# Stick-breaking attention with one mask pass, a scan on the minus log, and turned weights without zero blocks

## The chip, the cores and the metric

One Trainium2 chip, of which one core is used. The metric is the device time of one execution in microseconds (us). The kernel before was run three times: 2461.14, 2464.58 and 2466.43 us, median 2464.58 us. Engines are named as in the profile: PE is TensorE (PEld its weight loads), DVE is VectorE, ACT is ScalarE, POOL is GpSimd, SP issues the DMAs.

## The reference, cut to what matters

One transformer layer on 2048 tokens of 1024 channels: modulated RMS norm, a projection, three token mixers side by side (attention, causal pooling, spatial gating), an output projection, and a SwiGLU feed-forward part. The change is in the attention alone, which has 8 heads of 64 channels and a window of 512 keys:

```
z = einsum('bqhd,bkhd->bhqk', q_blk, k_blk) * scale
log_rest = where(valid, log_sigmoid(-z), 0.0)
later = cumsum(log_rest, axis=3, reverse=True) - log_rest
w = where(valid, exp(log_rest + z + later), 0.0)
out = einsum('bhqk,bkhd->bqhd', w, v_blk)
```

A key is valid for a query if it lies before it and at most 512 tokens back. `log_rest + z` is `log_sigmoid(z)`, so a weight is the chance of stopping at this key times the chances of having passed all later ones.

## The kernel before, in words

All matrix products are done on values split in a high and a low part, with three products each (`mm3`), or two in the attention, where high and low part stand beside or under each other in one operand. Tokens are worked in 4 groups of 512. First come the projections of each group (`proj_a`, `proj_b`), then for each group the output projection and the feed-forward part (`gate_up`, `down`), whose weights are loaded anew for each group, split on ACT (line 263) and on DVE or POOL (line 265).

The attention is a generator (`attention`) that runs along with this work from about 175 us to 1900 us: `weave` emits a step of it whenever a credit, fed by the estimated time of the products in front, reaches one. So its instructions stand between those of the projections and of the feed-forward part in the queues of all engines. The framework then orders each engine's queue by its own timeline model and places the waits. Each engine works its queue strictly in order.

A step of the attention is `att_front` for one tile of 128 queries: the scores (`z`, lines 674 to 679, PE), a copy to SBUF (`zc`, line 681, ACT), then `log(1 + exp(-|z|))` in three ACT instructions (lines 686 to 688), the sum with `max(z, 0)` (line 690, DVE), two masks of 128 columns on this (lines 693 and 698, POOL; the second only for groups 1 to 3), a scan from the last key to the first (line 704, DVE), the difference of scores and scan (line 707, DVE), the same two masks on that (POOL), and the exponential (line 709, ACT). A tile has 640 keys in groups 1 to 3, and 128 to 512 in group 0. There are 128 tiles: 96 of 640 keys and 8 of each smaller size.

`att_back` takes a pair of query tiles, one step later. It works in rounds of two blocks of 128 keys: the weights are turned by PE into the PSUM tile `tr` (line 735; there is one `tr`), copied by ACT as the high part (line 750), subtracted by DVE as the low part (line 751), and multiplied with the values into `av` (line 757), 256 columns at a time: two query tiles side by side. Where one of the two query tiles doesn't see a key block, its place in `wT` is filled with zeros by POOL (line 739). In such a round the used columns fall in two runs, and copy and subtraction are done once per run. A pair has three rounds in groups 1 to 3, and one or two in group 0: 168 rounds in all, of which 112 have two runs.

Of the kernel before, what the change touches and what calls it, by code (L numbers as in the profile page):

```python
# [9 lines left out]
F32 = mybir.dt.float32  # L10
# [5 lines left out]
P = 128  # L16
# [20 lines left out]
def tile_hybrid_trunk(  # L37
# [51 lines left out]
    def mm(ps, lhsT, rhs, start=True, stop=True):  # L89
        PE.matmul(ps, lhsT=lhsT, rhs=rhs, start=start, stop=stop)  # L90
# [40 lines left out]
    def sig_tail(y, e):  # L131
        """e <- log(1 + exp(-|y|)); y <- min(y, 0) - e; y <- exp(y) = sigmoid(y)."""
# [120 lines left out]
    cnt = [0]  # L253

    def wsplit(raw, hl):
        """hl[:, 0] + hl[:, 1] = raw, exactly."""
# [47 lines left out]
    def to_channels(xts, A, sh, res):  # L304
        """4 tiles [128 tok, 1024] -> 8 tiles [128 ch, hi/lo, 512 tok] of A * x + sh."""
# [20 lines left out]
    def ws_unit(ps, hl, hT):  # L326
        """weight-stationary: ps[128 out ch, 512 tok]."""
        for kc in range(KC):
            mm3(
                ps, (hl[:, 0, kc, :], hl[:, 1, kc, :]), (hT[kc][:, 0], hT[kc][:, 1]), 0, 0, kc == 0, kc == KC - 1  # L330
            )

    def seg_scale(raws, dim):
        """1/rms over the channels of raws (tiles [128 ch, 512]), on every partition."""
# [39 lines left out]
    def start():  # L374
        """h of group 0 and its first products, as sc1 and sh1 become known by quarters of the channels."""
# [101 lines left out]
    def proj_a(g):  # L477
        tok = slice(g * GT, (g + 1) * GT)
        hT = hTs[g]
        # q, k  # L480
# [24 lines left out]
        # v  # L505
# [27 lines left out]
        # pooling  # L533
# [130 lines left out]
    def att_front(g, h, i, qst, kst, koff):  # L664
        """weights of stick breaking of q tile i (of group g): [128 q, keys]."""
# [8 lines left out]
        for l in range(2):  # L674
# [5 lines left out]
        zc = st("zc", [P, 640])  # L680
        ACT.activation(
            out=zc[:, :n].rearrange("p (a b) -> p a b", a=pieces), in_=z[:, :pieces, :nn], func=AF.Copy
        )
        e = st("ee", [P, 640])[:, :n]
        zc = zc[:, :n]
# [3 lines left out]
        sp = e  # L689
        DVE.scalar_tensor_tensor(out=sp, in0=zc, scalar=0.0, in1=e, op0=ALU.max, op1=ALU.add)  # L690

        def masks(t, fill):
            POOL.affine_select(  # L693
# [416 lines left out]
```

## Time and profile before

| | |
|---|---|
| median of three runs | 2464.58 us |
| profiled execution: span from the first to the last instruction | 2463.7 us |
| PE busy | 2352.7 us, 95% |
| PEld busy | 1977.3 us, 80% |
| DVE busy | 1692.1 us, 69% |
| ACT busy | 1362.9 us, 55% |
| POOL busy | 1217.0 us, 49% |
| mean granted clock of PE | 0.986 of full speed |

Of the profiled execution the profile gives no time beside its span. A busy share is the union of an engine's instructions over the span. Matmuls are pipelined: one of 512 columns is listed with 395 ns, but in a row of them the next starts after about 0.23 us (22 in 5.28 us). So a price of a matmul is read from the distance of two starts, not from its listed length. "Idle before" names the instruction whose end released the waiting one.

### The profile page before, as it was taken

The page shows a single profiled execution, that of the slowest core. Times are in us where ns is not written, and L with a number is a line of the kernel's source. Part 1 is how long each engine was busy: PE and PEld are TensorE (multiplying, and loading weights), DVE is VectorE, ACT ScalarE, POOL GpSimd, SP SyncE. Part 2 cuts the span into 40 slices and gives each one's busy share as a digit, 9 for nine tenths or more (in the row PEclk, how much of TensorE's full clock was granted, in tenths as well). Part 3 has the DMA queues.
Part 4 walks back from the last instruction along what each step waited for, and adds up shares of the span by engine and source line. Part 5 has one row for each costly group of instructions (what it writes and reads, how often), then busy time and mean ns, then how long its engine had stood idle before and what let it go on. Part 6 is the DMA issues. An engine that isn't in the chain of part 4 may idle for free.

```text
span 2463.7 us, 32486 instructions
## 1 busy us (share of the span) xinstructions
PE 2352.7 (95%) x11730; PEld 1977.3 (80%) x11730; DVE 1692.1 (69%) x2125; ACT 1362.9 (55%) x2307; POOL 1217.0 (49%) x1157
## 2 busy tenths in 40 slices
PE   5999999999999999998999999889999999999998
PEld 4888979788788888777888888768788878788887
DVE  7577888767876777878877777877775456543435
ACT  5366767656666655656665655566664343433333
POOL 4142533345465455675554555754554456344445
PEclk8999999999999999999999999999999999999999
DMA  8857374554333333433433334334333343433332
GB/s 250 270 167 238 120 244 133 158 165 122 96 97 105 105 104 98 139 121 100 129 115 105 105 102 132 124 98 130 99 103 90 102 146 102 140 95 99 98 100 77
DMA packets 336512, 315.62 MB, mean 128 GB/s; under 512 B 12168, under 2 KB 267870, under 8 KB 336352
## 3 DMA queue, kind: packets, MB, share of 16 engines
q1 hardware_dynamic: 336352, 313.56, 41.3%
q8 instruction: 92, 1.51, 0.2%
q14 instruction: 68, 0.56, 0.1%
HBM read 279.95 MB, written 33.56 MB: 127 GB/s over the span
## 4 chain that ended last, share of the span: by engine, by line
PE 49%; DVE 18%; POOL 11%; issue 10%; ACT 8%; DMA 4%; SPq 1%; POOLq 0%; DVEq 0%; ACTq 0%
PE d L90 45%; POOL b L868 4%; DVE ee L704 3%; DVE hl L265 2%; DVE zc L707 2%; POOL hl L265 2%; PE av L90 2%; ACT hl L263 1%; DMA qst<-q_s 1%; DVE b L301 1%; PE tr L735 1%; DMA b<-in_w_ada_dram 1%; PE z L90 1%; DVE ee L690 1%; POOL b L916 1%
## 5 line engine op out<-in xcount | busy, mean ns | idle before, releaser
L90 PE MATMUL d<-b,hl 128*128 128x512 f32 x5184 | 1254.2, 395 | 8.3 <-DVE b L300 3.2
L90 PEld LDWEIGHTS d<-b,hl 128*128 128x128 f32 x5184 | 961.9, 189 | 208.2 <-DVE b L300 5.0
L90 PE MATMUL d<-hl,b 128*128 128x512 f32 (+1 forms) x4428 | 913.9, 359 | 13.2 <-DVE y L867 12.4
L90 PEld LDWEIGHTS d<-hl,b 128*128 128x128 f32 x4428 | 728.9, 191 | 128.3 <-DVE y L867 15.0
L263 ACT ACTIVATE hl<-raw 128x1024 fp32r<-128x1024 f32 x368 | 387.1, 1054 | 238.0 <-PE d L90 231.0
L265 POOL TENSOR_TENSOR hl<-raw,hl 128x1024 fp32r<-128x1024 f32 x122 | 308.2, 2527 | 325.1 <-ACT hl L263 308.7
L265 DVE TENSOR_TENSOR hl<-raw,hl 128x1024 fp32r<-128x1024 f32 x246 | 336.1, 1368 | 191.9 <-ACT hl L263 185.0
L868 POOL TENSOR_TENSOR b<-b,y 128x512 f32<-128x512 f32 x248 | 388.8, 1576 | 143.4 <-DVE y L867 135.8
L916 POOL TENSOR_TENSOR b<-y,b 128x512 fp32r<-128x512 f32 x88 | 165.0, 1875 | 228.3 <-DVE b L915 223.0
L704 DVE TENSOR_TENSOR_SCAN ee<-ee 128x640 f32<-128x640 f32 (+4 forms) x128 | 204.5, 1598 | 61.8 <-POOL ee L698 54.8
L867 DVE TENSOR_TENSOR y<-d,b 128x512 f32<-128x512 f32 x248 | 167.7, 681 | 91.4 <-PE d L90 88.9
L709 ACT ACTIVATE zc<-zc 128x640 f32<-128x640 f32 (+4 forms) x128 | 85.8, 670 | 257.5 <-POOL zc L698 223.4
L90 PE MATMUL av<-wT,vst 128*128 128x256 f32 x672 | 173.0, 295 | 30.6 <-DVE wT L751 13.4
L693 POOL TENSOR_SCALAR_AFFINE_SELECT zc<-zc 128x128 f32<-128x128 f32 x128 | 81.4, 636 | 221.9 <-DVE zc L707 213.8
L751 DVE TENSOR_TENSOR wT<-tr,wT 128x128 fp32r<-128x128 f32 (+1 forms) x280 | 116.6, 416 | 85.5 <-ACT wT L750 85.2
L90 PEld LDWEIGHTS av<-wT,vst 128*128 128x128 f32 x672 | 122.5, 192 | 59.7 <-DVE wT L751 21.4
L750 ACT ACTIVATE wT<-tr 128x128 fp32r<-128x128 f32 (+1 forms) x280 | 105.8, 378 | 104.4 <-DVE wT L751 71.2
L690 DVE SCALAR_TENSOR_TENSOR ee<-zc,ee 128x640 f32<-128x640 f32 (+4 forms) x128 | 125.5, 981 | 47.9 <-ACT ee L688 47.2
L693 POOL TENSOR_SCALAR_AFFINE_SELECT ee<-ee 128x128 f32<-128x128 f32 x128 | 53.6, 419 | 193.2 <-DVE ee L690 189.6
L907 ACT ACTIVATE y<-d 128x512 f32<-128x512 f32 x88 | 52.3, 594 | 150.8 <-PE d L90 150.7
L707 DVE TENSOR_TENSOR zc<-zc,ee 128x640 f32<-128x640 f32 (+4 forms) x128 | 133.7, 1044 | 2.4
L910 DVE SCALAR_TENSOR_TENSOR y<-d,y 128x512 f32<-128x512 f32 x88 | 60.3, 685 | 84.1 <-ACT y L909 83.7
(187 smaller groups left out, 2248.1 us busy)
## 6 DMA issues: line engine op xcount, KB each, us to landing
raw<-in_w_gate_up_dram SPq DMA_DIRECT2D x176, 512.0 KB, 3.9
raw<-in_w_down_dram SPq DMA_DIRECT2D x88, 512.0 KB, 3.7
raw<-in_w_in_dram SPq DMA_DIRECT2D x72, 512.0 KB, 5.2
b<-in_w_ada_dram SPq DMA_DIRECT2D x48, 512.0 KB, 6.7
raw<-in_w_out_dram SPq DMA_DIRECT2D x32, 512.0 KB, 4.3
b<-in_x_dram SPq DMA_DIRECT2D x28, 512.0 KB, 6.0
kst<-k_s SPq DMA_DIRECT2D x24, 512.0 KB, 4.1
qst<-q_s SPq DMA_DIRECT2D x64, 128.0 KB, 4.3
```

The source lines that it names most:

```text
L90: PE.matmul(ps, lhsT=lhsT, rhs=rhs, start=start, stop=stop)
L263: ACT.activation(out=h, in_=r, func=AF.Copy)
L265: eng.tensor_tensor(out=l, in0=r, in1=h.bitcast(F32), op=ALU.subtract)
L690: DVE.scalar_tensor_tensor(out=sp, in0=zc, scalar=0.0, in1=e, op0=ALU.max, op1=ALU.add)
L693: POOL.affine_select(out=t[:, n - P : n], in_=t[:, n - P : n], pattern=[[-1, P]], compare_op=ALU.is_ge, fill=fill, base=-1, channel_multip ...
L704: DVE.tensor_tensor_scan(out=e[:, ::-1], data0=sp[:, ::-1], data1=sp[:, ::-1], initial=0.0, op0=ALU.add, op1=ALU.bypass)
L707: DVE.tensor_tensor(out=zc, in0=zc, in1=e, op=ALU.subtract)
L750: ACT.activation(out=wT[:, 0, a:b], in_=tr[:, a:b], func=AF.Copy)
L751: DVE.tensor_tensor(out=wT[:, 1, a:b], in0=tr[:, a:b], in1=wT[:, 0, a:b].bitcast(F32), op=ALU.subtract)
L867: DVE.tensor_tensor(out=y, in0=ps, in1=gain[:, cs], op=ALU.mult)
L868: POOL.tensor_tensor(out=x1[t][:, cs], in0=x1[t][:, cs], in1=y, op=ALU.add)
L916: POOL.tensor_tensor(out=a[:, 1], in0=y, in1=a[:, 0].bitcast(F32), op=ALU.subtract)
```

## The change

- The masks are applied once, on the copied scores, before the first of the three ACT instructions, with -1e30 as fill.
- DVE makes `e = min(z, 0) - log(1 + exp(-|z|))`, the log of sigmoid(z), in place of the softplus. One scan then gives the minus log of the weight directly: each step adds the score of the next key and takes away `e` of this key. For this the scores stand in a tile with one more column, which POOL sets to zero (128 x 1), and the scan writes its result over the scores, one column to the right. The separate subtraction is gone, and the exponential has the factor -1.
- In `att_back` the key blocks that both query tiles see come first, with 256 columns, and the blocks that only one of them sees come last, with 128 columns. There are no zero blocks, and no memsets of `wT`. A round is filled up to 512 columns and copied by one ACT and one DVE instruction: of 512, 512 and 256 columns for a pair of groups 1 to 3 (48 pairs), of 384 or of 512 and 384 columns for a pair of group 0 (8 pairs each).

```diff
-    def mm(ps, lhsT, rhs, start=True, stop=True):
-        PE.matmul(ps, lhsT=lhsT, rhs=rhs, start=start, stop=stop)
+    def mm(ps, lhsT, rhs, start=True, stop=True, skip=False):
+        PE.matmul(ps, lhsT=lhsT, rhs=rhs, start=start, stop=stop, skip_group_check=skip)
...
-        zc = st("zc", [P, 640])
-        ACT.activation(
-            out=zc[:, :n].rearrange("p (a b) -> p a b", a=pieces), in_=z[:, :pieces, :nn], func=AF.Copy
+        zt = st("zc", [P, 641])
+        POOL.memset(zt[:, n : n + 1], 0.0)
+        zc = zt[:, :n]
+        ACT.activation(out=zc.rearrange("p (a b) -> p a b", a=pieces), in_=z[:, :pieces, :nn], func=AF.Copy)
+        POOL.affine_select(
+            out=zc[:, n - P : n], in_=zc[:, n - P : n], pattern=[[-1, P]], compare_op=ALU.is_ge, fill=NEG,
+            base=-1, channel_multiplier=1,
         )
+        if g > 0:
+            POOL.affine_select(
+                out=zc[:, 0:P], in_=zc[:, 0:P], pattern=[[1, P]], compare_op=ALU.is_ge, fill=NEG,
+                base=0, channel_multiplier=-1,
+            )
         e = st("ee", [P, 640])[:, :n]
-        zc = zc[:, :n]
         ACT.activation(out=e, in_=zc, func=AF.Abs)
         ACT.activation(out=e, in_=e, func=AF.Exp, scale=-1.0)
         ACT.activation(out=e, in_=e, func=AF.Ln, bias=1.0)
-        sp = e
-        DVE.scalar_tensor_tensor(out=sp, in0=zc, scalar=0.0, in1=e, op0=ALU.max, op1=ALU.add)
-
-        def masks(t, fill):
-            POOL.affine_select(
-                out=t[:, n - P : n], in_=t[:, n - P : n], pattern=[[-1, P]], compare_op=ALU.is_ge, fill=fill,
-                base=-1, channel_multiplier=1,
-            )
-            if g > 0:
-                POOL.affine_select(
-                    out=t[:, 0:P], in_=t[:, 0:P], pattern=[[1, P]], compare_op=ALU.is_ge, fill=fill,
-                    base=0, channel_multiplier=-1,
-                )
-
-        masks(sp, 0.0)
+        DVE.scalar_tensor_tensor(out=e, in0=zc, scalar=0.0, in1=e, op0=ALU.min, op1=ALU.subtract)
+        w = zt[:, 1 : n + 1]
         DVE.tensor_tensor_scan(
-            out=e[:, ::-1], data0=sp[:, ::-1], data1=sp[:, ::-1], initial=0.0, op0=ALU.add, op1=ALU.bypass
+            out=w[:, ::-1], data0=w[:, ::-1], data1=e[:, ::-1], initial=0.0, op0=ALU.add, op1=ALU.subtract
         )
-        DVE.tensor_tensor(out=zc, in0=zc, in1=e, op=ALU.subtract)
-        masks(zc, NEG)
-        ACT.activation(out=zc, in_=zc, func=AF.Exp)
-        return zc
+        ACT.activation(out=w, in_=w, func=AF.Exp, scale=-1.0)
+        return w
     def att_back(g, i0, wq, vst, av):
-        """av[:, pair] += [v_hi | v_lo]^T w^T for q tiles i0, i0 + 1."""
         if g > 0:
-            kts = list(range(i0, i0 + 6))
-            has = lambda kt, i: i <= kt <= i + 4
+            both, one = list(range(i0 + 1, i0 + 5)), [(i0, 0), (i0 + 5, 1)]
             loc = lambda kt, i: kt - i
         else:
-            kts = list(range(0, i0 + 2))
-            has = lambda kt, i: kt <= i
+            both, one = list(range(0, i0 + 1)), [(i0 + 1, 1)]
             loc = lambda kt, i: kt
-        nm = 2 * len(kts)
+        items = [(kt, (0, 1)) for kt in both] + [(kt, (q,)) for kt, q in one]
+        rounds, n = [], 512
+        for kt, qs in items:
+            if n + len(qs) * P > 512:
+                rounds.append([])
+                n = 0
+            rounds[-1].append((kt, qs, n))
+            n += len(qs) * P
         m = 0
-        for b0 in range(0, len(kts), 2):
-            bk = kts[b0 : b0 + 2]
+        for rd in rounds:
             seq[0] += 1
             tr = psa.tile([P, 512], F32, tag="tr", name=f"tr_{seq[0]}", bufs=1)
             wT = st("wT", [P, 2, 512], F32R)
-            lo_c, hi_c = None, None
-            for s, kt in enumerate(bk):
-                for q in range(2):
-                    i = i0 + q
-                    c0 = s * 256 + q * P
-                    if has(kt, i):
-                        PE.transpose(
-                            out=tr[:, c0 : c0 + P], in_=wq[q][:, loc(kt, i) * P : (loc(kt, i) + 1) * P], identity=ident
-                        )
-                    else:
-                        POOL.memset(wT[:, :, c0 : c0 + P].bitcast(F32), 0.0)
-            runs = []
-            for s, kt in enumerate(bk):
-                for q in range(2):
-                    if has(kt, i0 + q):
-                        c0 = s * 256 + q * P
-                        if runs and runs[-1][1] == c0:
-                            runs[-1][1] = c0 + P
-                        else:
-                            runs.append([c0, c0 + P])
-            for a, b in runs:
-                ACT.activation(out=wT[:, 0, a:b], in_=tr[:, a:b], func=AF.Copy)
-                DVE.tensor_tensor(
-                    out=wT[:, 1, a:b], in0=tr[:, a:b], in1=wT[:, 0, a:b].bitcast(F32), op=ALU.subtract
-                )
-            for s, kt in enumerate(bk):
+            for kt, qs, c0 in rd:
+                for j, q in enumerate(qs):
+                    b = loc(kt, i0 + q) * P
+                    w = c0 + (j + 1) * P
+                    PE.transpose(out=tr[:, w - P : w], in_=wq[q][:, b : b + P], identity=ident)
+            ACT.activation(out=wT[:, 0, :w], in_=tr[:, :w], func=AF.Copy)
+            DVE.tensor_tensor(out=wT[:, 1, :w], in0=tr[:, :w], in1=wT[:, 0, :w].bitcast(F32), op=ALU.subtract)
+            for kt, qs, c0 in rd:
+                w = len(qs) * P
+                o = (i0 + qs[0]) * P
                 for l in range(2):
-                    mm(
-                        av[:, (i0 % 4) * P : (i0 % 4) * P + 256], vst[:, kt, :],
-                        wT[:, l, s * 256 : (s + 1) * 256], m == 0, m == nm - 1,
-                    )
                     m += 1
+                    mm(av[:, o : o + w], vst[:, kt, :], wT[:, l, c0 : c0 + w], m == 1, m == 2 * len(items), True)
```

How the queues change is shown at three places. The first is PE at the last round of a pair of group 1; `av` is the sum of weights and values, `z` the scores of a later tile, `tr` the turned weights, and the other rows are other work. Before:

```order
L90 MATMUL z_6643<-kst_6282,qst_6284 128x320 x4
L90 MATMUL aux_6873<-b_6190,wsT 128x256 x2
L90 MATMUL av_5557<-wT_6530,vst_5554 128x256
L90 MATMUL z_6666<-kst_6282,qst_6284 128x320 x4
L90 MATMUL aux_6986<-b_6190,wsT 128x256 x2
L90 MATMUL av_5557<-wT_6530,vst_5554 128x256 x3
L735 MATMUL tr_6761<-ident,zc_6300 128x128 x2
L652 MATMUL aux_7168<-ident,b_5986 128x128 x4
```

And with the change:

```order
L90 MATMUL z_6519<-kst_6168,qst_6170 128x320 x2
L90 MATMUL aux_6739<-b_6076,wsT 128x256 x2
L90 MATMUL aux_6850<-b_6076,wsT 128x256 x2
L90 MATMUL av_5463<-wT_6410,vst_5460 128x128
L90 MATMUL z_6540<-kst_6168,qst_6170 128x320 x4
L652 MATMUL aux_7022<-ident,b_5878 128x128 x4
L90 MATMUL av_5463<-wT_6410,vst_5460 128x128 x3
L734 MATMUL tr_6633<-ident,zc_6186 128x128
```

The four products of the round stand in the same manner, one alone and three in a row, with 128 columns in place of 256.

The second place is ACT at the end of group 0, where `wT` of the last round of a pair is copied; line 778 (760 in the change) splits the queries of the next head as they land. Before:

```order
L687 ACTIVATE ee_4697<-ee_4697 128x512
L709 ACTIVATE zc_4588<-zc_4588 128x384
L750 ACTIVATE wT_4752<-tr_4751 128x256
L688 ACTIVATE ee_4697<-ee_4697 128x512
L778 ACTIVATE qst_4876<-qst_4876 128x512
L750 ACTIVATE wT_4752<-tr_4751 128x128
L498 ACTIVATE b_4795<-d_4770 128x512
L263 ACTIVATE hl_5015<-raw_5013 128x1024
```

And with the change, where line 683 is the copy of the scores, lines 695 to 697 are the three instructions on them, line 706 is the exponential and line 735 the copy of `wT`:

```order
L683 ACTIVATE zc_4622<-z_4619 128x512
L706 ACTIVATE zc_4516<-zc_4516 128x384
L695 ACTIVATE ee_4628<-zc_4622 128x512
L696 ACTIVATE ee_4628<-ee_4628 128x512
L735 ACTIVATE wT_4678<-tr_4677 128x384
L697 ACTIVATE ee_4628<-ee_4628 128x512
L760 ACTIVATE qst_4796<-qst_4796 128x512
L498 ACTIVATE b_4718<-d_4693 128x512
```

The copy of `wT` is one instruction, and it stands ahead of the split of the queries; before, its second half stood behind it.

The third place is POOL in group 1, over two tiles of the attention; line 868 (850 in the change) adds a product to the residual stream, line 265 is a weight split. Before:

```order
L265 TENSOR_TENSOR hl_5983<-raw_5981,hl_5983 128x1024
L868 TENSOR_TENSOR b_5495<-b_5495,y_5874 128x512
L693 AFFINE_SELECT ee_5819<-ee_5819 128x128
L698 AFFINE_SELECT ee_5819<-ee_5819 128x128
L868 TENSOR_TENSOR b_5497<-b_5497,y_5897 128x512
L693 AFFINE_SELECT zc_5817<-zc_5817 128x128
L698 AFFINE_SELECT zc_5817<-zc_5817 128x128
L868 TENSOR_TENSOR b_5499<-b_5499,y_5920 128x512
L868 TENSOR_TENSOR b_5501<-b_5501,y_5966 128x512
L693 AFFINE_SELECT ee_5937<-ee_5937 128x128
L698 AFFINE_SELECT ee_5937<-ee_5937 128x128
```

And with the change:

```order
L681 MEMSET zc_5713 128x1
L681 MEMSET zc_5829 128x1
L265 TENSOR_TENSOR hl_5875<-raw_5873,hl_5875 128x1024
L850 TENSOR_TENSOR b_5407<-b_5407,y_5742 128x512
L685 AFFINE_SELECT zc_5713<-zc_5713 128x128
L690 AFFINE_SELECT zc_5713<-zc_5713 128x128
L850 TENSOR_TENSOR b_5401<-b_5401,y_5768 128x512
L850 TENSOR_TENSOR b_5403<-b_5403,y_5791 128x512
L850 TENSOR_TENSOR b_5405<-b_5405,y_5814 128x512
L685 AFFINE_SELECT zc_5829<-zc_5829 128x128
L690 AFFINE_SELECT zc_5829<-zc_5829 128x128
```

A tile has two masks and a small memset in place of four masks, and the memset of the second tile stands ahead of the masks of the first.

## Rows read from the trace of the kernel before

**Rows 1.** The page's part on engines: busy us (share of the span), instructions.
```profile
PE 2352.7 (95%) x11730; PEld 1977.3 (80%) x11730; DVE 1692.1 (69%) x2125; ACT 1362.9 (55%) x2307; POOL 1217.0 (49%) x1157
```

**Rows 2.** Busy time of each engine in three stretches, granted TensorE clock, DMA share.
```profile
0.00:175.00 175.00, 139.84 (x775) 119.76 (x776) 111.93 (x152) 85.24 (x152) 57.64 (x73) 0.95 0.72 227
175.00:1900.00 1725.00, 1661.22 (x8511) 1401.83 (x8510) 1313.63 (x1647) 1073.05 (x1859) 894.49 (x931) 0.99 0.41 125
1900.00:2463.70 563.70, 551.59 (x2448) 455.72 (x2446) 266.57 (x327) 204.63 (x297) 264.91 (x153) 0.99 0.35 106
```

**Rows 3.** Waits of TensorE: line, for whom, us in total, times, longest.
```profile
PE av L90 <- DVE wT L751: 13.4, 14, 2.5
PE av L90 <- ACT wT L750: 13.2, 9, 3.6
PE d L90 <- DVE y L867: 12.4, 7, 3.8
...
PE z L90 <- ACT zc L681: 6.7, 5, 1.7
```

**Rows 4.** TensorE in order of time, three places: start, length, operation, count.
```profile
390.93 0.23 PE L90 MATMUL z<-kst,qst 128*128 128x128 f32 x1
390.99 0.45 PE L90 MATMUL d<-b,hl 128*128 128x512 f32 x1
...
438.71 0.34 PE L90 MATMUL z<-kst,qst 128*128 128x128 f32 x2
438.88 0.33 PE L90 MATMUL av<-wT,vst 128*128 128x256 f32 x1
...
1202.47 0.52 PE L90 MATMUL av<-wT,vst 128*128 128x256 f32 x3
```

**Rows 5.** The page's groups of instructions: busy us, mean ns of one, idle before.
```profile
L704 DVE TENSOR_TENSOR_SCAN ee<-ee 128x640 f32<-128x640 f32 (+4 forms) x128 | 204.5, 1598 | 61.8 <-POOL ee L698 54.8
...
L90 PE MATMUL av<-wT,vst 128*128 128x256 f32 x672 | 173.0, 295 | 30.6 <-DVE wT L751 13.4
...
L751 DVE TENSOR_TENSOR wT<-tr,wT 128x128 fp32r<-128x128 f32 (+1 forms) x280 | 116.6, 416 | 85.5 <-ACT wT L750 85.2
...
L750 ACT ACTIVATE wT<-tr 128x128 fp32r<-128x128 f32 (+1 forms) x280 | 105.8, 378 | 104.4 <-DVE wT L751 71.2
...
L693 POOL TENSOR_SCALAR_AFFINE_SELECT ee<-ee 128x128 f32<-128x128 f32 x128 | 53.6, 419 | 193.2 <-DVE ee L690 189.6
...
L707 DVE TENSOR_TENSOR zc<-zc,ee 128x640 f32<-128x640 f32 (+4 forms) x128 | 133.7, 1044 | 2.4
```

**Rows 6.** Groups by line with shapes apart, at lines 751, 739 and 698.
```profile
L751 DVE TENSOR_TENSOR wT<-tr,wT 128x256 fp32r<-128x256 f32 x112 | 46.6, 416 | 35.3 <-ACT wT L750 35.1
...
L751 DVE TENSOR_TENSOR wT<-tr,wT 128x512 fp32r<-128x512 f32 x56 | 38.1, 681 | 26.4 <-ACT wT L750 26.3
...
L739 POOL MEMSET wT<- 128x256 f32 x112 | 35.0, 312 | 23.9 <-PE av L90 22.2 <-PE tr L735 1.6
...
L698 POOL TENSOR_SCALAR_AFFINE_SELECT ee<-ee 128x128 f32<-128x128 f32 x96 | 33.2, 346 | 0.0
```

**Rows 7.** All engines in order of time, from 467.39 us on.
```profile
467.39 0.63 ACT L778 ACTIVATE qst<-qst 128x512 fp32r<-128x512 f32 x1 [6.11 <-DMA qst<-q_s]
467.93 0.26 ACT L750 ACTIVATE wT<-tr 128x128 fp32r<-128x128 f32 x1
...
468.24 0.38 PE L90 MATMUL av<-wT,vst 128*128 128x256 f32 x1 [3.57 <-ACT wT L750]
```

**Rows 8.** Waits of ScalarE: us in total, times, longest.
```profile
ACT zc L709 <- POOL zc L698: 223.4, 75, 8.8
...
ACT wT L750 <- DVE wT L751: 71.2, 52, 4.7
...
ACT zc L709 <- POOL zc L693: 34.0, 21, 7.0
...
ACT zc L681 <- PE tr L735: 28.4, 18, 5.0
```

## The prediction

> **What bounds the kernel now.** I read the page first: PE is busy 95% of the span, DVE 69%, POOL 49% [rows 1]. So the time is PE's instructions plus the 111 us in which PE stands still (2463.7 - 2352.7). Next I cut the span into three stretches to see where it stands still [rows 2]. Before the attention begins PE idles for 35.2 us of 175, after it for 12.1 us of 563.7, and the change touches neither. In the 1725 us that hold the attention PE idles for 63.8 us, and the mean granted clock is 0.99. The clock has two levels, 1.2 and 2.4 GHz, so 0.99 means that about 2% of this stretch, some 35 us, ran at the lower one, where about half of the time, some 17 us, is lost. DVE is busy for 1313.6 of these 1725 us (76%), POOL for 894.5, ACT for 1073.1: none of them is the bound, but PE waits for each at times. The list of PE's waits [rows 3] says for what: 13.4 us and 13.2 us for the turned weights wT (DVE's half and ACT's half), 6.7 us for the copy of the scores that frees z, and 12.4 us for DVE at line 867, where a product is taken out of PSUM. Thus the change can win in two ways: fewer columns on PE, and fewer waits behind the attention's work on ACT and DVE. Work taken from DVE or POOL alone is worth nothing while PE is busy.
>
> **PE's columns.** The 672 products av of 256 columns become 448 of 256 and 224 of 128: each of the 48 pairs of groups 1 to 3 gets four narrow ones (192), and each of the 16 pairs of group 0 two (32). The number of transposes and of weight loads is the same. Three av products of 256 columns take 0.52 us from the first start to the last end, and one lasts 0.28 us, so they start 0.12 us apart [rows 4]. (The mean of 295 ns in [rows 5] is a length, of which most lies beside the neighbours.) For 128 columns the trace has the score products of group 0: one alone is followed by the next product after 0.06 us (390.93 to 390.99), and two in a row take 0.17 us until the next starts (438.71 to 438.88), 0.06 for the first and 0.11 for the second [rows 4]. I take the second to be held by the weight load. In the changed order of PE the 224 stand 47 times alone, 47 times in threes, 16 times in twos and once in four, as in the place that is shown. That is 47 x 0.06 + 47 x 0.28 + 16 x 0.17 + 0.39 = 19.1 us, against 224 x 0.12 = 26.9 us: PE wins 7.8 us. The bounds are all at 0.11 (24.6, a gain of 2.3 us) and all at 0.06 (13.4, a gain of 13.5 us). I take 7.8, since both prices are of the same operation and the order gives the mix.
>
> The Trainium skill ("TensorE: Matmul & The Clock Gate", Back-to-back issue gap) has N/2.4 + 2.5 ns for a matmul alone, 56 ns for 128 columns, and (LDWEIGHTS) 107 ns for loading 128 columns of weights. The trace's 0.06 us agrees with the first and its 0.11 us with the second, so this page only warns that halving the columns below the load's time gives back less than half. By the gap alone the columns would give 14.3 us, and the time would be 2440 us; by the load alone 2.9 us, and it would be 2452.
>
> **The copies of wT.** Before, 112 of the 168 rounds copy two runs, and the ACT copy of the second run waits for DVE's subtraction of the first: 71.2 us of ACT's idle time, 52 times [rows 8]. So the second half passes two queues twice. What that costs PE is seen at 467.39 us: ACT is held for 6.11 us by the queries' DMA, the second copy of wT (128 columns) comes behind it, and PE stands still for 3.57 us until that is done [rows 7]. In the new order at that place there is one copy, ahead of the queries. If PE's 13.4 + 13.2 = 26.6 us for wT [rows 3] fell evenly on the rounds, two thirds (17.7 us) would be in rounds of two runs. A single copy can be late as well, so I take half of the 26.6 as gone: 13.3 us. The bounds are nothing (all waits come from the place of a copy in ACT's queue, which stays) and 17.7 us; below nothing, a wider copy lasts longer: DVE's instruction for 512 columns is 681 ns against 416 for 256 [rows 6], and where it stands last before PE that is up to 0.27 us a wait, 6 us for the 23 waits of [rows 3]. Shorter waits also leave the clock up; of the 17 us I take 2, with bounds of 0 and 8 (half).
>
> **DVE, POOL, ACT.** DVE loses line 707 wholly, 133.7 us [rows 5]. Of wT it had 116.6 us [rows 5]; now it has 104 instructions of 512 at 681 ns, 48 of 256 at 416 ns, and 16 of 384, for which I take the middle, 549 ns [rows 6]: 99.6 us, 17.0 less. POOL loses 53.6 us of masks [rows 5], 33.2 of masks and 35.0 of memsets [rows 6], and gets 128 memsets of one column. The trace has no such memset; between nothing and the 312 ns of the memset of 256 columns [rows 6] it is 0 to 40 us, and even the upper end leaves POOL with less. ACT has 168 copies for 280. All of this lies beside PE and I count it at nothing, but for the 12.4 us of line 867: DVE has 150.7 of 1313.6 us less to do, 11%, which is 1.4 us. The cover is PE's own work; were it gone, DVE's 150.7 us would show. The scan has a second operation (subtract) and reads two tiles in place of one twice. From the trace it may be dearer by nothing, or by up to as much again as the 204.5 us of all scans [rows 5], or somewhat cheaper since it no longer waits on masks; I take nothing, as both forms have two inputs and one state. At the upper end DVE would be busy for 1692 - 151 + 205 = 1746 us, still below PE. Neither SP's queue nor a DMA changes.
>
> **The waits that are added.** The first of the three ACT instructions now waits for the masks on POOL, one or no instruction behind the copy of the scores. Behind it in ACT's queue stand copies of wT and weight splits, for which DVE and then PE wait. The memset stands in POOL's queue ahead of a weight split and of additions to the residual stream, and waits until PE has turned the tile that had the buffer before; today ACT waits for that, 28.4 us in 18 waits [rows 8]. What goes is ACT's wait for the masks ahead of the exponential, 223.4 + 34.0 us [rows 8]: the exponential waits for the scan alone now. I expect the new waits of ACT to be shorter than the old ones in sum, but some will stand in a worse place. I put PE's loss at the 6.7 us that it waits for the scores' copy today [rows 3], once more; bounds: nothing, and 33.3 us (below).
>
> **The sum.** 7.8 + 13.3 + 2 + 1.4 - 6.7 = 17.8 us less than the profiled execution's span of 2463.7 us, which gives 2445.9. The median of the runs, 2464.58, lies 0.9 above that span, so 2446.8. I forecast 2447 us.
>
> **Rivals.** (a) *Only the columns count.* The waits for wT come from where ACT's queue stands, and the new order makes as many as it takes away. For it: in [rows 7] the DMA is the root, and it stays; against it: 52 waits of ACT for DVE that can't occur again. 2464.6 - 7.8 = 2457 us, and 2462 at the lower price of the columns.
>
> (b) *ACT is held behind POOL, and the kernel gets slower.* The place is the first ACT instruction behind the masks. POOL's queue holds instructions of more than a microsecond, and the masks wait behind them with ACT idle. This decides from the point where the wait, over 128 tiles, is more than the 223.4 + 34.0 + 71.2 = 328.6 us of ACT's waits that go [rows 8], 2.6 us a tile. Then all that PE waits for behind ACT (13.4 + 13.2 + 6.7 = 33.3 us [rows 3]) grows; doubled it costs 33.3 us, with the columns' 7.8 won: 2490 us. At half of that, 2473 us. For it: POOL is half busy and strictly in order. Against it: the waits of today have the same POOL queue in them, twice a tile.
>
> (c) *The relief is larger.* If all four waits of [rows 3] went (45.7 us), with 8 us of the clock and 7.8 us of columns, it would be 61.5 us: 2403. A quarter of the waits beyond my count (8 us) and 4 us more of the clock give 2435. Against it: those that remain hang on DMAs and on the feed-forward part.
>
> **How the numbers follow.** Forecast (2440 to 2454): 0.45. Rival (c): 0.16. Rival (a): 0.28, of which 0.17 end below 2459.7 (0.2%, 4.9 us, is what a measurement of this kernel can tell from no change) and 0.11 above. Rival (b): 0.11, of which 0.04 end near no change and 0.07 slower. So faster is 0.45 + 0.16 + 0.17 = 0.78, the same 0.15, slower 0.07. For 8 in 10 I leave out the far half of (c) and the slower part of (b): 2433 to 2464.
>
> **What would show it.** Right: av in two shapes, with PE's busy time down by about as many us as the columns give; no wait of ACT for line 751's successor; the two wT waits of PE together at about 13 us; no DVE wait for POOL ahead of the scan; idle time of PE from 175 to 1900 us at about 55 us. The steps fall if the 128 column products stand 0.11 us or more apart everywhere, if the waits for wT remain at 26 us, or if the scan's mean, 1598 ns [rows 5], has risen. The forecast is wrong if ACT's wait for the masks is over 2.6 us a tile, if PE has new waits above 20 us on any one line, or if the clock's mean in the stretch falls below 0.98.

## The result, and the profile after

The changed kernel takes 2440.28 us (median of 4 runs, 2433.14 to 2442.7), the kernel before on the same chip 2464.95 us: a ratio of 0.9893, 95% interval 0.9871 to 0.9916. That is 24.7 us less; 17.8 were forecast, and the time lies in the range (2433 to 2464), at the lower edge of the band that stood for the forecast itself (2440 to 2454). The terms of the sum are another matter.

The page's busy time, and the two stretches that answer to [rows 1, 2]:

```profile
PE 2345.3 (96%) x11730; PEld 1976.5 (81%) x11730; DVE 1554.4 (64%) x1885; ACT 1360.5 (56%) x2195; POOL 1090.3 (45%) x949
```

```profile
175.00:1900.00 1725.00, 1676.74 (x8619) 1420.47 (x8618) 1186.47 (x1420) 1080.95 (x1761) 775.16 (x724) 0.99 0.41 127
1900.00:2440.10 540.10, 528.04 (x2344) 436.23 (x2342) 257.38 (x314) 194.80 (x284) 257.92 (x150) 0.99 0.35 107
```

The span is 2440.1 us, 23.6 less. Of this 7.4 us are PE's busy time (2352.7 to 2345.3) and 16.2 us its idle time (111.0 to 94.8). The mean granted clock of the two profiled executions is 0.986 and 0.987; the four executions of the changed kernel have 0.984 to 0.990, so a gain by the clock of the 2 us that were forecast can't be told from none. DVE has 137.7 us less to do, POOL 126.7 us, ACT 2.4 us.

What PE waits for, answering to [rows 3]:

```profile
PE av L90 <- DVE wT L736: 16.8, 8, 4.3
PE av L90 <- ACT wT L735: 11.9, 7, 4.7
...
PE aux L90 <- DVE b L642: 3.7, 1, 3.7
...
PE d L90 <- DVE y L849: 3.4, 3, 2.2
...
PE tr L734 <- ACT zc L706: 3.2, 3, 2.2
...
PE z L90 <- ACT zc L683: 2.0, 2, 1.1
```

The two waits for wT (lines 736 and 735 now) are 28.7 us together, where they were 26.6: they did not shrink. The wait at line 849 (867 before) went from 12.4 to 3.4 us, that for the scores' copy from 6.7 to 2.0. The transposes wait 3.2 us for the exponential, and the spatial gating (line 642) has a wait of 3.7 us that was not there.

The groups, answering to [rows 5, 6]:

```profile
L703 DVE TENSOR_TENSOR_SCAN zc<-zc,ee 128x640 f32<-128x640 f32 x96 | 169.0, 1761 | 1.9
...
L90 PE MATMUL av<-wT,vst 128*128 128x256 f32 x448 | 96.7, 292 | 29.4 <-DVE wT L736 16.8 <-ACT wT L735 11.9 <-DVE av L785 0.6
...
L736 DVE TENSOR_TENSOR wT<-tr,wT 128x512 fp32r<-128x512 f32 x104 | 70.9, 682 | 21.5 <-ACT wT L735 21.4
...
L690 POOL TENSOR_SCALAR_AFFINE_SELECT zc<-zc 128x128 f32<-128x128 f32 x96 | 40.6, 423 | 0.1
...
L90 PE MATMUL av<-wT,vst 128*128 128x128 f32 x224 | 38.4, 254 | 0.0
...
L736 DVE TENSOR_TENSOR wT<-tr,wT 128x256 fp32r<-128x256 f32 x48 | 20.1, 419 | 24.7 <-ACT wT L735 24.6
...
L681 POOL MEMSET zc<- 128x1 f32 x128 | 11.2, 107 | 90.0 <-PE tr L734 70.9 <-issue 18.2
```

The scan with two operations lasts no longer than before: all 128 have a mean of 1532 ns against 1598 [rows 5]. A memset of one column is listed with 107 ns.

What ScalarE waits for, answering to [rows 8]:

```profile
ACT zc L706 <- DVE zc L703: 162.5, 88, 5.5
...
ACT ee L695 <- POOL zc L690: 128.2, 63, 5.7
...
ACT zc L683 <- PE tr L734: 48.8, 32, 4.7
...
ACT ee L695 <- POOL zc L685: 17.0, 16, 2.9
```

The exponential waits 162.5 us for the scan, and the first of the three instructions 128.2 + 17.0 = 145.2 us for the masks, 1.1 us a tile. Before, the exponential waited 257.4 us for the masks alone. No ACT copy of wT waits for DVE's subtraction any more (71.2 us before).

### The profile page after: what moved, and what is told of

It reads as the page before. It is cut to its first block, busy times and chain, and to the rows that moved or that the text cites. A ratio compares the mean times of both kernels' runs of the same rounds, so it can differ in the third digit from the quotient of the medians.

```text
span 2440.1 us, 31763 instructions
## 1 busy us (share of the span) xinstructions
PE 2345.3 (96%) x11730; PEld 1976.5 (81%) x11730; DVE 1554.4 (64%) x1885; ACT 1360.5 (56%) x2195; POOL 1090.3 (45%) x949
## 4 chain that ended last, share of the span: by engine, by line
PE 42%; DVE 4%; ACT 3%; issue 2%; POOL 2%; DMA 0%; SPq 0%; POOLq 0%; DVEq 0%; ACTq 0%
PE d L90 39%; PE av L90 1%; POOL b L850 1%; PE tr L734 1%; PE z L90 1%; DVE zc L703 1%; DVE hl L265 1%; ACT c L287 1%; ACT hl L263 0%; DVE ee L699 0%; DVE b L300 0%; POOL hl L265 0%; DVE y L849 0%; DVE b L301 0%; DMA b<-pg_s 0%
## 5 line engine op out<-in xcount | busy, mean ns | idle before, releaser
L850 POOL TENSOR_TENSOR b<-b,y 128x512 f32<-128x512 f32 x248 | 379.7, 1541 | 188.8 <-DVE y L849 178.7
L703 DVE TENSOR_TENSOR_SCAN zc<-zc,ee 128x640 f32<-128x640 f32 (+4 forms) x128 | 196.2, 1532 | 2.5
L699 DVE SCALAR_TENSOR_TENSOR ee<-zc,ee 128x640 f32<-128x640 f32 (+4 forms) x128 | 116.9, 914 | 126.1 <-ACT ee L697 122.7
L706 ACT ACTIVATE zc<-zc 128x640 f32<-128x640 f32 (+4 forms) x128 | 86.0, 672 | 162.7 <-DVE zc L703 162.5
L695 ACT ACTIVATE ee<-zc 128x640 f32<-128x640 f32 (+4 forms) x128 | 85.8, 670 | 146.9 <-POOL zc L690 128.2
L90 PE MATMUL av<-wT,vst 128*128 128x256 f32 (+1 forms) x672 | 132.5, 279 | 29.4 <-DVE wT L736 16.8
L90 PEld LDWEIGHTS av<-wT,vst 128*128 128x128 f32 x672 | 112.6, 191 | 52.8 <-DVE wT L736 21.2
L736 DVE TENSOR_TENSOR wT<-tr,wT 128x512 fp32r<-128x512 f32 (+1 forms) x168 | 99.8, 594 | 51.8 <-ACT wT L735 51.6
L685 POOL TENSOR_SCALAR_AFFINE_SELECT zc<-zc 128x128 f32<-128x128 f32 x128 | 66.7, 521 | 143.3 <-ACT zc L683 143.1
L892 DVE SCALAR_TENSOR_TENSOR y<-d,y 128x512 f32<-128x512 f32 x88 | 60.4, 687 | 100.5 <-ACT y L891 100.1
L683 ACT ACTIVATE zc<-z 128x640 f32<-128x640 f32 (+4 forms) x128 | 80.8, 631 | 61.8 <-PE tr L734 48.8
L90 PE MATMUL z<-kst,qst 128*128 128x320 f32 (+1 forms) x448 | 100.3, 324 | 3.0 <-ACT zc L683 2.0
```

Of the source, the lines that this page charges most:

```text
L90: PE.matmul(ps, lhsT=lhsT, rhs=rhs, start=start, stop=stop, skip_group_check=skip)
L683: ACT.activation(out=zc.rearrange("p (a b) -> p a b", a=pieces), in_=z[:, :pieces, :nn], func=AF.Copy)
L695: ACT.activation(out=e, in_=zc, func=AF.Abs)
L699: DVE.scalar_tensor_tensor(out=e, in0=zc, scalar=0.0, in1=e, op0=ALU.min, op1=ALU.subtract)
L703: DVE.tensor_tensor_scan(out=w[:, ::-1], data0=w[:, ::-1], data1=e[:, ::-1], initial=0.0, op0=ALU.add, op1=ALU.subtract)
L706: ACT.activation(out=w, in_=w, func=AF.Exp, scale=-1.0)
```

## The experiments

Each time is a median. The kernel before was run beside each group of runs, at 2464.3, 2463.3 and 2461.8 us; intervals are of the ratio to it. In the diffs a minus stands before lines of the changed kernel, or, for the order alone, of the kernel that is named.

**The two halves apart: the new sums on the old weights, and the new weights on the old sums.** Both are given in short: the first in words, the second by a few of its lines.

```diff
 # e1_back: att_front as before, att_back as changed
-        masks on zc; e = min(zc, 0) - e; scan of zc and e; exp(-w)
+        e = max(zc, 0) + e; masks on e; scan of e; zc = zc - e; masks on zc; exp(zc)
 # e2_front: att_front as changed, att_back as before
-        both, one = list(range(i0 + 1, i0 + 5)), [(i0, 0), (i0 + 5, 1)]
+            kts = list(range(i0, i0 + 6))
+                        POOL.memset(wT[:, :, c0 : c0 + P].bitcast(F32), 0.0)
```

Expected of the first: 

> The weighted sums of the change (no zero blocks, 128 wide columns, one copy per round) with the old weights (masks twice, scan and subtraction). By the prediction's terms: columns 7.8 us, waits for wT 13.3 us and clock 2 us are won here, so 2464.9 - 23.1 = 2442 us, with the two wT waits of TensorE at 13 us in sum. By the theory formed after the result (the waits for wT don't shrink; what shrank are the waits on VectorE at the product's exit and on the score copies, and VectorE loses only 17 us here): columns 7.8 and about 1 us, 2456 us, wT waits about 27 us.

Expected of the second: 

> The weights of the change (masks on the scores alone, scan on the minus log, no subtraction) with the old weighted sums (zero blocks, two copies in split rounds). By the prediction's terms (1.4 us won at line 867, 6.7 us lost at the masks): 2464.9 + 5.3 = 2470 us. By the theory after the result (VectorE's 134 us and GpSimd's 87 us less give TensorE shorter waits outside wT): about 16 us won, 2449 us, with TensorE's busy time unchanged at 2352 us.

The new sums alone took 2448.8 us (0.9933, 0.992 to 0.9945), 15.5 us less. The new weights alone took 2432.12 us (0.9872, 0.9859 to 0.9886), 32.2 us less: more than the whole change, and outside both forecasts for it; 2448.8 lies between the two that were made for the first. PE's waits for wT in the first and in the second:

```profile
PE av L90 <- DVE wT L739: 15.9, 15, 3.4
...
PE d L90 <- DVE y L852: 9.5, 6, 2.2
PE av L90 <- ACT wT L738: 8.6, 8, 2.2
```

```profile
PE av L90 <- ACT wT L747: 13.6, 6, 5.0
...
PE z L90 <- ACT zc L683: 6.9, 4, 3.1
PE d L90 <- DVE y L864: 4.8, 4, 2.2
...
PE av L90 <- DVE wT L748: 4.0, 5, 3.0
```

With single copies they are 24.5 us (15.9 + 8.6), with the copies of before 17.6 us (13.6 + 4.0). So single copies don't shorten these waits. The weights, which the prediction had put down as a loss of 5.3 us, are the larger half. The two halves don't add up: on top of the new sums the new weights bring 8.5 us (2448.8 to 2440.3), and not 32.2.

**The columns.** In the changed kernel the 224 narrow products are made 256 wide again.

```diff
-                w = len(qs) * P
-                o = (i0 + qs[0]) * P
+                wide = 2 * P
+                o = i0 * P
+                c1 = min(c0, w - wide)
-                    mm(av[:, o : o + w], vst[:, kt, :], wT[:, l, c0 : c0 + w], m == 1, m == 2 * len(items), True)
+                    mm(av[:, o : o + wide], vst[:, kt, :], wT[:, l, c1 : c1 + wide], m == 1, m == 2 * len(items), True)
```

Expected: 

> The changed kernel with 256 columns in each of the 224 products that it made 128 wide; what lies beside the block in wT is added to the other query tile too, so the sums are not the reference's, and only the columns' time is asked for. If the columns are worth what the prediction says: 2440.3 + 7.8 = 2448 us, with TensorE's busy time up by 7 to 8 us to 2353 us. If narrow columns are held by the weight load: 2442 us. If other waits hide them: 2440 us.

It took 2442.02 us (0.9914, 0.9901 to 0.9928), 1.7 us more than the changed kernel, and PE's busy time rose by 1.4 us:

```profile
PE 2346.7 (96%) x11730; PEld 1975.8 (81%) x11730; DVE 1552.0 (64%) x1885; ACT 1361.2 (56%) x2195; POOL 1088.6 (45%) x949
```

The two intervals overlap, so the time shows 1.7 us and not 7.8. The trace says where the rest is. I took for each product av the distance from its start to the next matmul's, less the waits between: the 672 take 91.6 us in the kernel before, 78.6 in the changed one, and 86.7 in this run, 8.1 more than in the changed one. With the new weights on the old sums, where they are wide too, they take 86.6. The products d, which this run leaves as they are, take 7.0 us less in this run than in the changed kernel (2073.4 and 2080.4). So the narrow columns are worth what was forecast, and the rest of PE's work moved by as much the other way.

**The order alone.** Three kernels with the attention's credit begun at one half, all else the same.

```diff
-    credit = [0.0]
+    credit = [0.5]
```

Expected of the changed kernel: 

> The changed kernel with the attention's credit begun at one half: every step of the attention is emitted half a step earlier, the work is the same. It asks how much of a difference is the order alone. If the gain lies in the work removed: within 4 us of 2440. If it lies in a lucky order: 8 us or more away, 2448 us or above.

Expected of the new weights with the old sums: 

> The changed weights with the old weighted sums (2432 us with the old start), also with the credit begun at one half. If the new weighted sums cost 8 us on top of the new weights by what they do, this is again some 8 us below the run of the whole change with the same start. If those 8 us are the order, the two are within 4 us of each other, or the other way round.

Expected of the kernel before: 

> The kernel before, with the credit begun at one half. If the order alone moves the time by less than the effects discussed: 2460 to 2469 us. If the order is worth as much as the change: 2450 or less, or 2475 or more.

The kernel before went from 2463.3 to 2473.02 us (1.0032, 1.0022 to 1.0043), the new weights with the old sums from 2432.1 to 2444.48, the changed kernel from 2440.3 to 2438.24. So the order alone moves these three by up to 12 us (and another, below, by 14), and two kernels that differ by less can't be told apart by one order. PE's busy time moves with it: 2340.7 and 2347.7 us for the new weights with the old sums, by as much as the 7.4 us between the kernel before and the changed one. Over both starts the kernel before has 2468 to 2469 us, the new weights with the old sums 2438, and the whole change 2439: on the old sums the new weights are worth about 30 us, and the new sums on top of them nothing that these runs can show; the new sums alone were run with one start only. In the changed kernel with the other start the waits for wT are 13.8 us, near the 13.3 that were forecast, and the time is the same, 2 us less for 15 us of waits:

```profile
PE d L90 <- DVE y L849: 8.5, 6, 2.5
PE av L90 <- DVE wT L736: 7.9, 8, 1.9
PE d L90 <- DVE y L894: 6.0, 5, 2.0
PE av L90 <- ACT wT L735: 5.9, 6, 2.5
```

**One copy or several.** The changed kernel with each round copied in parts of 256 columns.

```diff
+            for c in range(0, w, 256):
+                z = min(c + 256, w)
+                ACT.activation(out=wT[:, 0, c:z], in_=tr[:, c:z], func=AF.Copy)
+                DVE.tensor_tensor(out=wT[:, 1, c:z], in0=tr[:, c:z], in1=wT[:, 0, c:z].bitcast(F32), op=ALU.subtract)
```

Expected: 

> The changed kernel, but each round of turned weights is copied in parts of 256 columns (ACT, then VectorE, then the next part) in place of one copy of up to 512. If the wider copy is what holds the waits for wT up (28.7 us in sum against 17.6 with the old weighted sums on the new weights): the waits fall to about 18 us and the time to about 2432 us. If one copy is better, as the prediction has it: 2440 us or more, with waits of 29 us or more.

2436.16 us (0.9888, 0.9873 to 0.9903), with waits for wT of 18.5 us:

```profile
PE av L90 <- ACT wT L737: 9.5, 7, 5.2
PE av L90 <- DVE wT L738: 9.0, 9, 2.9
```

The waits are those that the first reading forecast, but single copies with the other start have 13.8 us, so the run doesn't bear that reading out. The time is 4 us below the changed kernel, within what the order does. No gain of one copy per round is seen here.

**A spare VectorE instruction per tile.**

```diff
         ACT.activation(out=w, in_=w, func=AF.Exp, scale=-1.0)
+        DVE.tensor_tensor(out=e, in0=e, in1=e, op=ALU.subtract)
```

Expected: 

> The changed kernel with one more VectorE instruction per tile, of the length of the removed subtraction (128 x n, about 1 us), whose result nobody needs, after the scan and beside the exponential. It gives VectorE back about 125 us and leaves the chain of a tile as it is. If VectorE's load is what the waits of TensorE shrank with: 9 to 13 us back, 2450 to 2453 us, with the wait at line 849 at 8 us or more. If it is the shorter chain of a tile (two mask passes and the subtraction gone between score and weight): within 4 us of 2440.

2483.24 us (1.0085, 1.0071 to 1.0098): 43 us more than the changed kernel, and 19 more than the kernel before, although DVE is less busy than there:

```profile
PE 2358.0 (95%) x11730; PEld 1979.7 (80%) x11730; DVE 1682.2 (68%) x2013; ACT 1359.7 (55%) x2195; POOL 1113.8 (45%) x949
```

So the sum of VectorE's work is not the measure: 1682.2 us here against 1692.1 [rows 1]. Neither reading had forecast so much. Of the 38.8 us by which the profiled span grew (2440.1 to 2478.9), 12.7 are PE's busy time, for the same matmuls, and 26.1 its idle time (94.8 to 120.9). The mean granted clock is 0.983, against 0.987 in the changed kernel; over the span that makes some 10 us, by my estimate, so about a quarter of the loss came by the clock. The waits for wT grew from 28.7 to 39.0 us, more of it behind ACT's half than behind DVE's:

```profile
PE av L90 <- DVE wT L737: 20.1, 15, 4.3
PE av L90 <- ACT wT L736: 18.9, 10, 5.9
```

**The masks without the scan.** The changed kernel with the old scan and subtraction, with both starts.

```diff
-        DVE.scalar_tensor_tensor(out=e, in0=zc, scalar=0.0, in1=e, op0=ALU.min, op1=ALU.subtract)
-            out=w[:, ::-1], data0=w[:, ::-1], data1=e[:, ::-1], initial=0.0, op0=ALU.add, op1=ALU.subtract
+        DVE.scalar_tensor_tensor(out=e, in0=zc, scalar=0.0, in1=e, op0=ALU.max, op1=ALU.add)
+            out=e[:, ::-1], data0=e[:, ::-1], data1=e[:, ::-1], initial=0.0, op0=ALU.add, op1=ALU.bypass
+        DVE.tensor_tensor(out=zc, in0=zc, in1=e, op=ALU.subtract)
```

Expected: 

> The changed kernel with the old scan and the old subtraction, and the masks on the scores alone: of the new weights the mask part only (the softplus of a masked score is zero without a second mask). VectorE has 134 us more than in the changed kernel, GpSimd about the same. If VectorE's load is what decides: 2460 to 2483 us (the run with a spare VectorE instruction per tile took 2483). If the masks out of the chain and off GpSimd are what decides: 2444 us or less.

Expected with the credit begun at one half: 

> The same with the attention's credit begun at one half, to tell the effect from the order (which moved the same work by up to 12 us). By VectorE's load: 2458 us or more again. By the masks: 2444 us or less.

2491.07 us (1.0112, 1.0094 to 1.0131) and 2477.19 us (1.0066, 1.0046 to 1.0087). So the masks' move alone makes the kernel slower: 42 and 28 us above the new sums on the old weights (2448.8, run with one start), which differ from this by the masks and the order only. The first time lies above the range that was forecast by DVE's load, the second in its range. With the subtraction then gone into the scan it is 51 and 39 us faster.

```profile
PE 2362.1 (95%) x11730; PEld 1980.2 (80%) x11730; DVE 1688.6 (68%) x2013; ACT 1358.3 (55%) x2195; POOL 1101.8 (44%) x821
```

```profile
ACT ee L693 <- POOL zc L688: 157.2, 71, 6.4
...
ACT ee L693 <- POOL zc L683: 22.5, 22, 2.9
```

DVE is as busy as with the new sums alone (1688.6 against 1686.7 us). ACT's wait for the masks is 157.2 + 22.5 = 179.7 us, 1.4 us a tile: 34.5 us more than the 145.2 of the changed kernel, and well under 2.6 us a tile.

**Masks put back on POOL.**

```diff
         ACT.activation(out=w, in_=w, func=AF.Exp, scale=-1.0)
+        POOL.affine_select(out=e[:, n - P : n], in_=e[:, n - P : n], ...)
+        if g > 0:
+            POOL.affine_select(out=e[:, 0:P], in_=e[:, 0:P], ...)
```

Expected: 

> The changed kernel with 224 masks put back on GpSimd at the end of a tile, on values that nobody reads any more. It gives GpSimd back about 87 us and no engine waits for it but for the buffer. If GpSimd's load matters: 8 us or more above 2440. If it lies beside PE and only VectorE's counts: 2436 to 2446 us.

2445.12 us (0.9933, 0.9915 to 0.9952), 4.8 us more than the changed kernel, or about 10 by the ratios to the kernel before beside each (0.9933 against 0.9893). Both lie within what the order does, so no cost of POOL's load is shown, and a small one is not excluded. POOL was 76.5 us busier (1166.8 against 1090.3).

**A zero column that stays.** The scores in three fixed tiles, the result of the scan over `e`.

```diff
-        zt = st("zc", [P, 641])
-        POOL.memset(zt[:, n : n + 1], 0.0)
+        zt = zts[zn[0] % 3]
+        if g == 0 or zn[0] < 35:
+            POOL.memset(zt[:, n : n + 1], 0.0)
-        w = zt[:, 1 : n + 1]
+        z1 = zt[:, 1 : n + 1]
+        w = e
```

Expected: 

> A version meant to be faster: the scores stand in three fixed tiles whose last column stays zero (35 memsets in place of 128), the scan writes over the log sigmoid, of which there are five buffers. GpSimd then has no memset that waits for TensorE's transposes (70.9 us in the changed kernel). If those waits cost TensorE time: 2430 us or less. If they lie beside it: 2434 to 2444 us.

2448.91 us (0.9947, 0.9928 to 0.9966): no gain, and above both forecasts. But this version doesn't take away what it was meant to. In the changed kernel POOL waits 70.9 us for transposes ahead of its memsets; here the 35 memsets that are left wait nearly as long, for the scan that last read the fixed tile:

```profile
POOL zc L685 <- DVE ee L709: 60.6, 17, 9.4
```

So what those waits cost stays open.

**Where the 30 to 50 us lie.** For each trace I counted the stretches of DVE in which instructions of the attention's weights (sum or difference with the log, scan, subtraction, spare one) follow each other with less than 0.15 us between, and summed those of over 3 us:

| kernel | time, us | DVE busy, us | stretches over 3 us: count, us | PE idle, us | of it under these instructions, us |
|---|---|---|---|---|---|
| new weights, old sums; start at one half | 2432; 2444 | 1564; 1584 | 16, 58; 23, 82 | 90.3; 100.5 | 8.2; 7.9 |
| changed; start at one half | 2440; 2438 | 1554; 1577 | 21, 81; 19, 68 | 94.8; 97.8 | 11.2; 6.8 |
| copies in parts | 2436 | 1568 | 17, 64 | 92.2 | 7.4 |
| wide columns | 2442 | 1552 | 22, 83 | 93.7 | 10.7 |
| masks put back on POOL | 2445 | 1550 | 19, 74 | 98.7 | 11.0 |
| zero column that stays | 2449 | 1559 | 16, 56 | 98.5 | 11.0 |
| new sums, old weights | 2449 | 1687 | 24, 87 | 99.9 | 8.8 |
| before; start at one half | 2464; 2473 | 1692; 1709 | 29, 106; 38, 141 | 111.0; 114.7 | 11.1; 19.8 |
| masks alone; start at one half | 2491; 2477 | 1689; 1701 | 52, 203; 58, 231 | 126.7; 119.9 | 19.7; 21.5 |
| spare VectorE instruction | 2483 | 1682 | 51, 204 | 120.9 | 26.9 |

Time is the median; the other columns are of the profiled execution. PE's idle time is the span less its busy time, and the last column is the part of PE's waits during which DVE works on one of these instructions.

The slow kernels are those with long stretches; the zero column that stays doesn't fit (56 us, and 2449). The line of 3 us helps in this: at their usual lengths three such instructions of 640 keys in a row take about 3.1 us (0.82, 1.49 and 0.82) and two 2.3. The last column doesn't depend on it. Of the 26.1 us that the spare instruction adds to PE's idle time, 15.7 lie under these instructions (11.2 to 26.9). But of the 16.2 us that the change took off PE's idle time none do (11.1 before, 11.2 after) with one start, and 13.0 of 16.9 (19.8 and 6.8) with the other. So these stretches cost PE time in the kernels with three instructions in a row, and they aren't all of it; the gain of the change itself is not shown to be theirs.

How such a stretch reaches PE is seen in the run with the spare instruction. The rows are in order of time, with start, length and engine; the wT of ACT is what DVE's wT needs:

```profile
1251.35 2.38 POOL L265 TENSOR_TENSOR hl<-raw,hl 128x1024 fp32r<-128x1024 f32 x1 [6.42 <-ACT hl L263]
...
1251.79 2.62 DVE L699 SCALAR_TENSOR_TENSOR ee<-zc,ee 128x640 f32<-128x640 f32 x1
1251.79 0.58 ACT L736 ACTIVATE wT<-tr 128x512 fp32r<-128x512 f32 x1
...
1254.45 1.49 DVE L703 TENSOR_TENSOR_SCAN zc<-zc,ee 128x640 f32<-128x640 f32 x1
1255.86 0.67 DVE L737 TENSOR_TENSOR wT<-tr,wT 128x512 fp32r<-128x512 f32 x1
...
1256.58 0.62 PE L90 MATMUL av<-wT,vst 128*128 128x256 f32 x3 [3.56 <-DVE wT L737]
```

ACT has its half of wT ready at 1252.37 us. DVE has just begun the difference for a tile, and works the scan behind it; its half of wT ends at 1256.53, and PE has stood still for 3.56 us. The spare instruction itself isn't ahead of it here: the stretch is a difference, lengthened beside POOL's split, and a scan. The same place in the changed kernel:

```profile
1224.83 0.82 DVE L699 SCALAR_TENSOR_TENSOR ee<-zc,ee 128x640 f32<-128x640 f32 x1
...
1225.12 2.76 POOL L265 TENSOR_TENSOR hl<-raw,hl 128x1024 fp32r<-128x1024 f32 x1 [6.42 <-ACT hl L263]
...
1225.56 0.58 ACT L735 ACTIVATE wT<-tr 128x512 fp32r<-128x512 f32 x1
...
1225.68 3.55 DVE L703 TENSOR_TENSOR_SCAN zc<-zc,ee 128x640 f32<-128x640 f32 x1
...
1229.15 0.66 DVE L736 TENSOR_TENSOR wT<-tr,wT 128x512 fp32r<-128x512 f32 x1
...
1229.87 0.62 PE L90 MATMUL av<-wT,vst 128*128 128x256 f32 x3 [2.64 <-DVE wT L736]
```

Here the scan alone takes 3.55 us, where its median is 1.49: it lies beside a weight split of 2.76 us on POOL. In the kernel before, masks stood between the sum and the scan, and DVE could do other work meanwhile; that this gap is what kept the kernel before from being as slow as the masks alone is my reading, and no run shows it. That POOL holds such instructions up, as here, isn't what sets the slow kernels apart: counting the instructions of 640 keys that last over 0.2 us more than their median, it added 87 us in the kernel before, 86 with the new sums alone, 83 with the spare instruction, 78 with the masks alone, and 46 in the changed kernel.

## Why the prediction was right or wrong

*Bound by PE, with two sources of gain:* right. Busy time gave 7.4 us and idle time 16.2. That the 7.4 come so near the 7.8 of the columns is in part luck, as the order alone moves the busy time by 7.0.

*Columns, 7.8 us:* right in mechanism and size. The distances agree with [rows 4]: leaving out those over 0.4 us, a narrow product is followed after 0.089 us in the mean (223 of 224), a wide one after 0.128 (444 of 448). Of the narrow ones 107 stand at 0.06 us and 101 at 0.11, near the mix that was forecast. Made wide again they took 8.1 us more of PE; the time shows 1.7 of it, as other work moved the other way.

*Copies of wT, 13.3 us:* wrong, and the prediction's own sign, waits for wT that remain at 26 us, says so. (Of the clock's 2 us nothing can be told.) The step that failed is that PE's waits for wT "fell evenly on the rounds, two thirds (17.7 us) would be in rounds of two runs", with half of 26.6 us gone by the single copy. The waits are 28.7 us after, 24.5 with the new sums alone, 17.6 with the old sums on the new weights, and 13.8 with another start; with two copies and that start they are 22.7 us in the kernel before and 19.4 with the new weights. So they move with the order by up to 15 us, and not with the number of copies. Splitting the copies again cost nothing, and at 13.8 us the time was the same as at 28.7.

*DVE at line 867, 1.4 us:* right in kind, too small. I sized it by DVE's share of work, 11%. The wait fell by 9.0 us (12.4 to 3.4), and by 6.6 with the other start (15.1 to 8.5). Once the masks are moved, the removal of line 707 was worth 39 to 51 us against the kernel that keeps it. The sentence "Work taken from DVE or POOL alone is worth nothing while PE is busy" is what misled: 128 us more of DVE work cost 43 us with PE 95% busy. In part PE's matmuls wait for short DVE instructions that stand in one queue behind long ones (15.7 of the 26.1 us of idle time in that run lie under such work), in part the clock fell; the rest is open.

*Waits added, 6.7 us lost:* the place was right, the loss isn't seen. PE's wait for the scores' copy, put at 6.7 us once more, fell from 6.7 to 2.0. ACT's wait for masks is 1.1 us a tile, under the 2.6 us from which rival (b) would decide. But the masks' move does cost 28 to 42 us when the subtraction stays. DVE's instructions of a tile then come with nothing between, which is a likely cause; ACT's longer wait for the masks (34.5 us more than in the changed kernel), which is rival (b), isn't excluded as part of it.

*Scan no dearer, memset between 0 and 40 us, POOL and ACT at nothing:* the first two right (1532 ns; 11.2 us). POOL's masks put back cost 4.8 to 10 us, inside the order's spread; ACT's load was not tried.

So the sum came out near by luck, by errors that cancel: 13.3 us of copies that were not there, against 6.7 us of loss that weren't there either and shorter waits elsewhere, of which 1.4 us were counted. Rival (c), a larger relief, was nearer in kind than the forecast.

What isn't shown: that the long stretches themselves are the cause was not tried by moving them apart with the same work, and the zero column that stays speaks against their being all of it. The fastest kernel seen is the new weights with the old sums, 2432 us; with the other start it took 2444, so it is not shown to beat the changed kernel by more than the order does.

## What to carry to other kernels

Work on an engine that is 69% busy can still cost the time of a kernel whose PE is 95% busy, here in part by what stands in its queue ahead of a short instruction that PE needs: price an instruction removed from such a queue by trying it, not by its share. A wait inside a chain may serve as the gap in which other work gets through, so removing the wait without the work behind it can cost; this is a reading that fits these runs, not a proof. Where a scheduler sets the order, try each candidate with a second start before believing a difference of less than about 0.6 per cent (14 us here).

## What the runs showed of the hardware

DVE instructions with two inputs in SBUF grow beside POOL's two-input ones: the scan of 640 took 3.55 us in place of 1.49 beside a split of 2.76 us on POOL, and the difference at 1251.79 us 2.62 in place of 0.82, beside a split that ran from 1251.35 to 1253.73 us. The Trainium skill ("SBUF — State Buffer", Who interferes with whom) says that a DVE instruction with two SBUF inputs and a GpSimd instruction that reads SBUF exclude each other for a whole instruction; both cases agree: 2.06 and 1.80 us were added, where 2.20 and 1.94 us of the split were left when the DVE instruction began. It is so throughout: in the changed kernel 43 of the 192 differences and scans of 640 keys last over 0.2 us more than their median, all 43 began while such an instruction of POOL ran, and each grew by what was left of it less 0.14 to 0.15 us. I had not expected this to be what PE waits for at wT.
